# A 31-tap causal convolution on VectorE: 27 of its shifts made 1024 tokens wide, and its work spread anew beside the projections

## The chip, the cores and the metric

The program runs on one core of one Trainium2 chip. The metric is the device time of one execution in microseconds (us); of several executions the median counts. Engines are named as the profile names them: PE (TensorE products), PEld (its weight loads), DVE (VectorE), ACT (ScalarE), POOL (GpSimd), SP (SyncE, which here issues loads).

## The reference

The program computes a first block (a mixer of convolution, pooling and attention, then a mixture of experts) and a second block of two layers, on 1024 tokens of width 1024. The change touches the start of the first block alone:

```python
h = rms_norm(x, attn_norm_g)
z = h @ w_in
a_val, a_gate, p_in, q, k, v = split(z)
# convolution branch, 256 channels
u = a_val * sigmoid(a_gate)
y = depthwise_conv(u, w_dw, width=31, causal) + b_dw
y = silu(layer_norm(y, ln_g, ln_b))
y_conv = y @ w_pw + b_pw
# pooling branch, 256 channels: window sums of 2, 4, 8, 16 tokens
y_pool = pool_mixer(p_in)
# attention branch: q and k are normalised per head, then differential attention over q, k, v
mix = concat([y_conv, y_pool, attention(q, k, v)])
x = x + mix @ w_out
```

All matrix products are made of three products of high and low parts (a weight is split into `wh`, rounded, and `wl`, the rest; an activation into `mh` and `ml`).

## The kernel before

**Convolution.** Channels lie on the 128 partitions, tokens along the row, so the 256 channels are two tiles (j = 0, 1) of 128 x 1024. `conv_taps` (L638 to L658) walks over two halves of 512 tokens. A half begins with one `tensor_scalar` per channel tile (L650, shift 0 and bias); then 30 shifts follow, each a `scalar_tensor_tensor` per channel tile (L656) that adds u, moved by the shift and scaled by the tap's weight, to y. That is 4 instructions of L650 and 120 of L656, all on DVE. A shift with both its instructions is one stage of the generator: 62 stages in all.

**What is woven into what.** The program is written as generators. `_weave(main, side, steps)` (L262) takes `steps` steps of the side work after each step of the main work. Three parts of `build` matter (L2196 to L2203):

- `conv_pool`, through `group` and `partT` (L469), makes the first products `psT`: six weight tiles (two for the values of the convolution, two for its gate, two for the pooling input) by token blocks of 256, 256 and 512. The gate's sigmoid (L564 to L568, ACT and DVE in turn) and its product with the values (L635) give `u`.
- 14 stages of the taps are woven into the last part of those products, 1.3 after each step.
- `qkv` then makes the values `psV` (8 tiles of 24 products, L500) and the queries and keys `psQ` (n = 0 to 3, each 8 groups of 24 products, normalised by L777, L507 and L780, transposed as `psQT` by L787 and written by L796 and L797). Beside it, 3.4 steps after each of its steps, run the other 48 tap stages, with `pool_out` mixed into them at 0.55 steps each, and after both `conv_norm`.

`pool_out` makes the window sums with copies and adds on POOL (L669, L670) and their scaling on DVE (L676 to L680). `conv_norm` does the layer norm and silu of y in two halves: products with ones (`psM` L710, `psS` L578), then ACT and DVE in turn. `conv_out` splits y into `csh` (ACT, L450) and `csl` (L446 through `low`, on DVE or POOL) and multiplies it (`psC`); it is woven into the start of the attention (`psD`, L880 on DVE, exponentials L885 on ACT, L890 on POOL, L891 on DVE, `psAT` L901).

**Weights.** SP loads a weight tile into one of four raw buffers, ACT rounds it (`wh`, L450), and `low` (L442) takes the rest on DVE, every third one on POOL (`wl`, L446). The first group of queries reads four weight tiles; the low part of the second, `wl`, is its 15th product.

**The order.** The order of instructions on each engine is set when the program is built, by a scheduler that takes the written order and the dependencies; each engine then works through its queue strictly in that order. What stands behind a waiting instruction waits too.

Of the kernel before, what the change touches and what calls it, by code (L numbers as in the profile page):

```python
# [14 lines left out]
OP = mybir.AluOpType  # L15
# [241 lines left out]
def _run(g):  # L257
    for _ in g:
        pass


def _weave(main, side, steps=1.0):  # L262

    due = 0.0
    for _ in main:
        yield
        due += steps
        while due >= 1.0:
            due -= 1.0
            if next(side, _END) is not _END:  # L270
                yield
    yield from side


def _some(gen, n):

    for _ in range(n):
        if next(gen, _END) is _END:
            return
        yield  # L280


def _chain(*gens):
    for g in gens:
        yield from g
# [31 lines left out]
class _Kernel:  # L317
# [321 lines left out]
        yield from self.group(lead, [  # L639
            lambda t0, n, j=j, use=use: self.partT(("c", j), self.hm, use, t0, n=n) for j, use in enumerate(uses)])  # L640

    def conv_taps(self):

        nc = self.nc
        us = self.us
        ys = self.ys = [self.d("cy") for _ in range(2)]
        for half in range(2):
            lo, hi = 512 * half, 512 * half + 512
            for j in range(2):
                nc.vector.tensor_scalar(ys[j][:, lo:hi], us[j][:, lo:hi], self.col(("cw", j), 30), self.col("cb", j),  # L650
                                        op0=OP.mult, op1=OP.add)
            yield
            for sh in range(1, 31):
                a = max(lo, sh)
                for j in range(2):
                    nc.vector.scalar_tensor_tensor(ys[j][:, a:hi], us[j][:, a - sh:hi - sh], self.col(("cw", j), 30 - sh),  # L656
                                                   ys[j][:, a:hi], op0=OP.mult, op1=OP.add)
                yield  # L658

    def pool_out(self):  # L660
# [1357 lines left out]
    def second_layer(self, i, lead):  # L2018
# [6 lines left out]
        values = self.gla_v(i)  # L2025
        yield from _some(values, 8)
        yield from _weave(_chain(
            values, self.gla_gate(i, 1), self.gla_qk(i, 2), self.gla_qk(i, 3),
            self.gla_gate(i, 2), self.gla_gate(i, 3), self.mla_gate(i, 0), self.mla_gate(i, 1), self.mla_c(i, "ckv"),
            _weave(self.mla_c(i, "cq"), self.mla_norm(i), 0.5), self.mla_gate(i, 2), self.mla_gate(i, 3)),  # L2030
            heads, 1.06)
        self.hm = None
        self.ahead = 1
        yield from self.mla_rope_in(i)
        yield from _weave(self.mla_nope(i), _chain(self.rope(i), self.mla_factor(i)), 1.2)
        self.ahead = 0
        attention = self.mla_attention(i)
# [131 lines left out]
    def build(self):  # L2169
        nc = self.nc  # L2170
        keys = [("c", j) for j in range(6)]
        keys += [("cp",)] + [("v1", 0, kq) for kq in range(4)] + [("n1", n, kh) for n in range(4) for kh in range(2)]
        keys += [("o1", n, kq) for n in range(2) for kq in range(4)]
        keys += [("pp", 0, nh) for nh in range(2)]
        keys += [("m", p, g) for p in PLACES for g in range(6)]
        keys += [("pp", 1, nh) for nh in range(2)]
        for i in range(LAYERS):
            keys += [("k0", i), ("qk", i, 0), ("gg", i, 0), ("qk", i, 1)]
            keys += [("gv", i, 0, kq) for kq in range(4)]
            keys += [("gg", i, 1), ("qk", i, 2), ("qk", i, 3), ("gg", i, 2), ("gg", i, 3)]  # L2180
            keys += [("ga", i, 0), ("ga", i, 1)]
            keys += [("ckv", i, j) for j in range(2)] + [("cq", i, j) for j in range(3)]
            keys += [("ga", i, 2), ("ga", i, 3)]
            keys += [("uq", i, j) for j in (2, 0, 1)] + [("uk", i), ("uv", i)]
            keys += [(n, i, c, kq) for n in ("o2", "pg") for c in range(2) for kq in range(4)]
        self.order(keys)


        lead = self.first_in()
        lead.step()  # L2190
        lead.step()
        lead.step()
        self.pre(1)
        lead.step()
        self.pre(2)
        self.ahead = 2  # L2196
        first = self.conv_pool(lead)
        _run(_some(first, 6))
        self.lambdas()
        _run(_some(first, 7))  # L2200
        taps = self.conv_taps()
        _run(_weave(first, _some(taps, 14), 1.3))
        self.ahead = 1  # L2203
        _run(_weave(self.qkv(), _chain(_weave(taps, self.pool_out(), 0.55), self.conv_norm()), 3.4))
        if self.stop == "qkv":
            return
        self.ahead = 0
        self.spare_rows()
        attention = _weave(self.diff_attention(), self.conv_out(), 1.0)
        _run(_some(attention, 39))  # L2210
        self.router_setup()
        order = OUT_ORDER
        self.fill_ycp(order[0] // 2)

        def fill(t):
            n = order.index(t)
            if n % 2 == 0 and n < 6:
                self.fill_ycp(order[n + 2] // 2)
        self.pp = self.tc.dram_tile([LAYERS, S, D], F32, name="pp")
        self.later = []  # L2220
        side = self.ple_proj(0, 4)

        def products():
            self.pre(8)
            for half, t in self.out_proj(("o1",), self.io["x"], self.after_first, order, fill, True):
                if (half, t) == (1, order[5]):
                    self.rope_tables()
                    self.make_masks()
                if (half, t) == (0, order[6]):
                    self.choose_most()  # L2230
                if (half, t) == (1, order[-1]):
                    self.ple_load(0)
                    self.pre(1)
                if (half, t) == (0, order[-1]):
                    _run(_some(side, 1))
                yield
        _run(_weave(attention, products(), 1.0))
        self.route(lambda n: _run(_some(side, n)))
        experts = self.experts()
        next(experts)  # L2240
        _run(side)
        if self.stop == "route":
            return
        self.ahead = 0
        for u, n in experts:
            if u == 8:
                self.overflow_rows()
            if u == n - 4:
                self.ple_load(1)
            if u == n - 2:  # L2250
                self.ahead = 1
            if u == n - 1:
                outs = [self.d("ppo") for _ in range(NT)]
                for o in outs:
                    nc.gpsimd.memset(o[:, 0:1], 0.0)
                side = self.ple_proj(1, outs=outs)
                _run(_some(side, 2))
                self.pool_every = 3
        self.overflow()
        lead = self.second_in()  # L2260
        lead.step()
        _run(_some(side, 6))
        lead.step()
        lead.step()
        _run(_some(side, 3))
        lead.step()
        _run(_some(side, 3))
        lead.step()
        _run(_some(side, 2))
        if self.stop == "moe":  # L2270
            lead.need(NT)
            return

        self.x_in = self.x2
        for i in range(LAYERS):
            self.ahead = 2
            _run(self.layer_in(i, lead))
            _run(self.second_layer(i, lead))
            lead = self.lead
            if self.stop == f"l{i}":  # L2280
                return
# [28 lines left out]
```

## Time and profile before

| | us |
|---|---|
| median of 3 runs | 2265.68 (2257.85 to 2266.74) |
| the profiled execution, its own time | 2266.57 |
| its span in the profile | 2264.8 |
| PE busy | 2130.3 (94%) |
| DVE busy | 1488.8 (66%) |
| ACT busy | 1154.4 (51%) |
| POOL busy | 495.9 (22%) |

The span runs from the first to the last instruction that the profile shows; 1.8 us of the execution's time lie around it. The busy shares are averages over the whole program; the part that the change touches is the stretch from about 65 to 300 us of the span, some 10% of it.

### The profile page before, as it was taken

How to read it: one execution, taken by the hardware profiler on the slowest of the kernel's cores; microseconds unless marked ns; L12 is line 12 of the kernel's file. 1: busy time of each engine (PE TensorE's matmuls, PEld its weight loads, DVE VectorE, ACT ScalarE, POOL GpSimd, SP SyncE). 2: the span in 40 equal slices, each digit the busy share in tenths (PEclk: the TensorE clock that was granted, in tenths of full speed). 3: DMA queues.
4: the chain of work that ended last, by engine and by line, in shares of the span. 5: the costliest groups of instructions: out<-in, count | busy, mean ns of one | idle time of the engine just before them, and what ended most of it. 6: DMA issues, size and time to landing. Idle time of an engine off the chain costs nothing.

```text
span 2264.8 us, 31148 instructions
## 1 busy us (share of the span) xinstructions
PE 2130.3 (94%) x11660; PEld 1805.5 (80%) x11660; DVE 1488.8 (66%) x2534; ACT 1154.4 (51%) x2184; POOL 495.9 (22%) x431
## 2 busy tenths in 40 slices
PE   7989888998999989999899999999999989999998
PEld 7878777786887768887688988888877877898886
DVE  5995788577788733576756674566267665675455
ACT  5314778435677655354444553356354444554344
POOL 1320143202232211112322341101021232332100
PEclk9999999999999999999999999999999999999999
DMA  5101231638999971011022024444001113013343
GB/s 199 47 19 57 75 84 33 215 118 284 283 326 325 269 232 63 19 47 66 29 75 56 10 75 159 165 153 143 10 29 56 47 66 84 10 43 135 121 150 130
DMA packets 78446, 255.09 MB, mean 113 GB/s; under 512 B 9680, under 2 KB 16976, under 8 KB 78288
## 3 DMA queue, kind: packets, MB, share of 16 engines
q1 hardware_dynamic: 65024, 205.84, 26.2%
q0 software_dynamic: 10672, 38.00, 7.2%
q10 hardware_dynamic: 2592, 9.18, 1.1%
q8 instruction: 94, 1.54, 0.3%
q14 instruction: 64, 0.52, 0.1%
HBM read 183.51 MB, written 58.98 MB: 107 GB/s over the span
## 4 chain that ended last, share of the span: by engine, by line
PE 65%; DVE 18%; DMA 6%; ACT 5%; issue 4%; POOL 1%; POOLq 0%; DVEq 0%; SPq 0%; ACTq 0%
PE psR L500 19%; PE psT L469 14%; PE psS L459 6%; PE psO L459 5%; DVE cy L656 4%; PE psV L500 4%; DMA raw<-in_wm_dram 3%; PE psG L1292 3%; PE psQ L500 3%; PE psPT L1968 2%; DVE wl L446 2%; PE psY L459 2%; PE psX L549 1%; ACT wh L450 1%; PE psMV L459 1%
## 5 line engine op out<-in xcount | busy, mean ns | idle before, releaser
L469 PE MATMUL psT<-mh,wh 128*128 128x512 f32 (+1 forms) x784 | 292.4, 373 | 9.5 <-ACT k L1568 4.1
L469 PE MATMUL psT<-ml,wh 128*128 128x512 f32 (+1 forms) x784 | 288.7, 368 | 2.1 <-DVE ml L558 2.1
L469 PE MATMUL psT<-mh,wl 128*128 128x512 f32 (+1 forms) x784 | 287.7, 367 | 0.0
L446 DVE TENSOR_TENSOR wl<-raw,wh 128x1024 fp32r<-128x1024 f32 x171 | 222.6, 1308 | 54.1 <-ACT wh L450 52.1
L450 ACT ACTIVATE wh<-raw 128x1024 fp32r<-128x1024 f32 x205 | 214.8, 1055 | 67.0 <-DMA raw<-in_wm_dram 29.3
L469 PEld LDWEIGHTS psT<-mh,wh 128*128 128x128 f32 x784 | 153.1, 195 | 35.4 <-ACT k L1568 4.8
L446 POOL TENSOR_TENSOR wl<-raw,wh 128x1024 fp32r<-128x1024 f32 x34 | 87.7, 2581 | 415.4 <-ACT wh L450 370.7
L469 PEld LDWEIGHTS psT<-ml,wh 128*128 128x128 f32 x784 | 152.8, 195 | 24.8 <-DVE ml L558 3.1
L469 PEld LDWEIGHTS psT<-mh,wl 128*128 128x128 f32 x784 | 152.8, 195 | 23.1
L500 PE MATMUL psR<-wh,mixh 128*128 128x512 f32 x384 | 152.3, 397 | 2.6 <-DVE mpT L1973 1.7
L500 PE MATMUL psR<-wh,mixl 128*128 128x512 f32 x384 | 149.9, 390 | 0.9 <-POOL mixl L446 0.9
L500 PE MATMUL psR<-wl,mixh 128*128 128x512 f32 x384 | 149.9, 390 | 0.0
L1956 POOL TENSOR_SCALAR mp<-mp,mrr 128x512 f32<-128x512 f32 x128 | 92.6, 736 | 213.1 <-DVE mrr L1954 191.7
L1952 ACT ACTIVATE mp<-psS,mnm,rq 128x1024 f32<-128x1024 f32 x64 | 77.4, 1209 | 83.3 <-DVE mnm L1949 83.2
L500 PE MATMUL psR<-wl,mh 128*128 128x512 f32 (+1 forms) x264 | 101.3, 384 | 1.2 <-DVE wl L446 1.2
L500 PE MATMUL psR<-wh,mh 128*128 128x512 f32 (+1 forms) x264 | 102.0, 386 | 0.0
L500 PE MATMUL psR<-wh,ml 128*128 128x512 f32 (+1 forms) x264 | 101.0, 383 | 0.0
L557 ACT ACTIVATE mh<-psX 128x256 fp32r<-128x256 f32 (+1 forms) x144 | 60.9, 453 | 77.3 <-PE psX L549 72.3
L459 PEld LDWEIGHTS psO<-mpT,mv 128*128 128x128 f32 x768 | 96.4, 191 | 2.6
L1947 DVE TENSOR_REDUCE mmx<-psS 128x1 f32<-128x1024 f32 x64 | 78.1, 1220 | 29.1 <-PE psS L459 29.0
L459 PE MATMUL psO<-mpT,mv 128*128 128x256 f32 x768 | 97.1, 283 | 0.0
L987 DVE TENSOR_TENSOR xr<-psR,xr 128x512 f32<-128x512 f32 x48 | 33.0, 690 | 94.2 <-PE psR L500 78.6
(498 smaller groups left out, 5665.3 us busy)
## 6 DMA issues: line engine op xcount, KB each, us to landing
raw<-in_wg_dram SPq DMA_DIRECT2D x109, 512.0 KB, 3.5
raw<-in_wm_dram SPq DMA_DIRECT2D x96, 512.0 KB, 6.2
pp<-ppo ACTq DMA_DIRECT2D x16, 512.0 KB, 7.5
h<-xr SPq DMA_DIRECT2D x16, 512.0 KB, 2.8
xr<-h SPq DMA_DIRECT2D x16, 512.0 KB, 4.8
ppr<-pp SPq DMA_DIRECT2D x16, 512.0 KB, 5.8
xt<-in_x_dram SPq DMA_DIRECT2D x8, 512.0 KB, 11.2
xr<-in_x_dram SPq DMA_DIRECT2D x8, 512.0 KB
```

Source lines behind the costliest of these rows:

```text
L446: e.tensor_tensor(out, full, high.bitcast(F32), op=OP.subtract)
L450: self.nc.scalar.activation(h, src, AF.Copy)
L459: self.nc.tensor.matmul(out, a, b, start=j == 0, stop=j == n - 1)
L469: self.nc.tensor.matmul(ps, p[:, a], q, start=k == 0 and j == 0, stop=k == nk - 1 and j == 2)
L500: self.nc.tensor.matmul(out, p, q[:, b], start=k == 0 and j == 0, stop=k == 7 and j == 2)
L557: nc.scalar.activation(h, v, AF.Copy)
L656: nc.vector.scalar_tensor_tensor(ys[j][:, a:hi], us[j][:, a - sh:hi - sh], self.col(("cw", j), 30 - sh), ys[j][:, a:hi], op0=OP.mult, op1= ...
L1292: self.nc.tensor.matmul(pg, m[x][:, k], w[:, b], start=k == 0 and n == 0, stop=k == 7 and n == 2)
L1947: nc.vector.tensor_reduce(mx, ps, axis=AX.X, op=OP.max)
L1952: nc.scalar.activation(p, ps, AF.Exp, bias=nm, scale=self.rq[0][:, t:t + 1], accum_out=sm)
L1956: nc.gpsimd.tensor_scalar(p[:, b], p[:, b], rr, 1.0, op0=OP.mult, op1=OP.mult)
L1968: nc.tensor.transpose(pt[:, a, 128 * n:128 * n + 128], p[:, 256 * c + 128 * a:256 * c + 128 * a + 128], self.ident)
```

## The change

The taps of a half keep their 512 tokens only for shift 0 and the shifts 1 to 3. The 27 shifts 4 to 30 become one instruction each per channel tile, 1020 to 994 tokens wide, and each of these 54 instructions is a stage of its own. Only 4 stages (shift 0 to 3 of the first half) are woven into the first products, 0.4 after each step, instead of 14. All others lie beside `qkv`: 2.6 steps after each of its first 8 steps (the values) and 3.5 after each later one, with `pool_out` at 0.5.

```diff
 def _weave(main, side, steps=1.0):
 
     due = 0.0
-    for _ in main:
+    for n, _ in enumerate(main):
         yield
-        due += steps
+        due += steps(n) if callable(steps) else steps
...
-    def conv_taps(self):
+    def conv_taps(self, early):
...
-        for half in range(2):
-            lo, hi = 512 * half, 512 * half + 512
+
+        def tap(j, sh, lo, hi):
+            a = max(lo, sh)
+            nc.vector.scalar_tensor_tensor(ys[j][:, a:hi], us[j][:, a - sh:hi - sh], self.col(("cw", j), 30 - sh),
+                                           ys[j][:, a:hi], op0=OP.mult, op1=OP.add)
+        for lo, hi in ((0, 512), (512, 1024)):
...
-            for sh in range(1, 31):
-                a = max(lo, sh)
+            for sh in range(1, early):
                 for j in range(2):
...
+                    tap(j, sh, lo, hi)
+                yield
+        for sh in range(early, 31):
+            for j in range(2):
+                tap(j, sh, 0, 1024)
                 yield
...
-        taps = self.conv_taps()
-        _run(_weave(first, _some(taps, 14), 1.3))
+        taps = self.conv_taps(4)
+        _run(_weave(first, _some(taps, 4), 0.4))
         self.ahead = 1
-        _run(_weave(self.qkv(), _chain(_weave(taps, self.pool_out(), 0.55), self.conv_norm()), 3.4))
+        _run(_weave(self.qkv(), _chain(_weave(taps, self.pool_out(), 0.5), self.conv_norm()),
+                    lambda n: 2.6 if n < 8 else 3.5))
```

Lines of the changed kernel behind L640 stand six further on; its taps are L650 and its shift 0 is L654. Three places show what moves in the built order. In the names, `cy` is y, `wl` a weight's low part, `pd` and `ps` belong to the pooling, the number tells one buffer from another.

First, DVE beside the first products, around the gate's sigmoid (L565, L567, L635) of the last 512 tokens. Before:

```order
L656 SCALAR_TENSOR_TENSOR cy_738<-u_158,cols_85,cy_738 128x500
L565 TENSOR_SCALAR u_157<-u_157 128x512
L656 SCALAR_TENSOR_TENSOR cy_737<-u_157,cols_85,cy_737 128x499
L656 SCALAR_TENSOR_TENSOR cy_738<-u_158,cols_85,cy_738 128x499
L567 SCALAR_TENSOR_TENSOR u_157<-u_157,psT_771 128x512
L446 TENSOR_TENSOR wl_921<-raw_917,wh_919 128x1024
L446 TENSOR_TENSOR wl_927<-raw_923,wh_925 128x1024
```

With the change:

```order
L650 SCALAR_TENSOR_TENSOR cy_764<-u_158,cols_85,cy_764 128x509
L446 TENSOR_TENSOR wl_901<-raw_897,wh_899 128x1024
L446 TENSOR_TENSOR wl_907<-raw_903,wh_905 128x1024
L565 TENSOR_SCALAR u_157<-u_157 128x512
L567 SCALAR_TENSOR_TENSOR u_157<-u_157,psT_767 128x512
L635 TENSOR_TENSOR u_157<-aval_155,u_157 128x512
L654 TENSOR_SCALAR cy_763<-u_157,cols_85 128x512
```

Ahead of the gate stand 6 taps instead of 24, the two weight splits come before the gate, and nothing stands between the gate's steps.

Second, DVE around the two weight splits that the first queries need. Before:

```order
L656 SCALAR_TENSOR_TENSOR cy_737<-u_157,cols_85,cy_737 128x512
L676 SCALAR_TENSOR_TENSOR pd_969<-ps_1142,pin_160 64x1008
L680 TENSOR_TENSOR pd_969<-pf_1176,pin_160 64x16
L446 TENSOR_TENSOR wl_1218<-raw_1214,wh_1216 128x1024
L446 TENSOR_TENSOR wl_1224<-raw_1220,wh_1222 128x1024
L676 SCALAR_TENSOR_TENSOR pd_969<-ps_1209,pin_160 64x1008
L656 SCALAR_TENSOR_TENSOR cy_738<-u_158,cols_85,cy_738 128x512
```

With the change:

```order
L650 SCALAR_TENSOR_TENSOR cy_763<-u_157,cols_85,cy_763 128x1000
L446 TENSOR_TENSOR wl_1170<-raw_1166,wh_1168 128x1024
L446 TENSOR_TENSOR wl_1176<-raw_1172,wh_1174 128x1024
L682 SCALAR_TENSOR_TENSOR pd_975<-ps_1248,pin_160 64x1008
L650 SCALAR_TENSOR_TENSOR cy_764<-u_158,cols_85,cy_764 128x1005
L650 SCALAR_TENSOR_TENSOR cy_763<-u_157,cols_85,cy_763 128x999
L650 SCALAR_TENSOR_TENSOR cy_764<-u_158,cols_85,cy_764 128x1004
L783 TENSOR_REDUCE qss_1209<-qsq_1207 128x4
```

Between the gate's first L635 and these splits stand 2 of L654, 6 half-width and 36 wide taps (before, between the gate's L567 and the splits, 2 of L650 and 67 half-width taps), the last 17 of them without a break; behind the splits 18 wide taps are left (before 27 half-width ones), 13 of them ahead of the eighth query tile. One scaling of the pooling (L682, which reads a sum from POOL) moves from ahead of the splits to right behind them, and the two splits for n = 1 move to ahead of the eighth query tile.

Third, ACT at the end of `qkv`, where `conv_out` begins. Before, the second half of `conv_norm` has ended 27 rows earlier:

```order
L796 ACTIVATE ql_2325<-psQT_2667,cols_85 64x256
L796 ACTIVATE ql_2327<-psQT_2654,cols_85 64x256
L796 ACTIVATE qh_2326<-psQT_2667,cols_85 64x256
L796 ACTIVATE ql_2327<-psQT_2667,cols_85 64x256
L450 ACTIVATE csh_2707<-cy_737 128x1024
L450 ACTIVATE csh_2711<-cy_738 128x1024
L885 ACTIVATE at_2695,few_2689<-at_2695,few_2689 128x1024
```

With the change:

```order
L802 ACTIVATE ql_2240<-psQT_2585,cols_85 64x256
L566 ACTIVATE sg_2610<-sg_2610,sm_83 128x512
L566 ACTIVATE sg_2619<-sg_2619,sm_83 128x512
L568 ACTIVATE sg_2610<-sg_2610 128x512
L568 ACTIVATE sg_2619<-sg_2619 128x512
L891 ACTIVATE at_2641,few_2635<-at_2641,few_2635 128x1024
L891 ACTIVATE at_2648,few_2635<-at_2648,few_2635 128x1024
L450 ACTIVATE csh_2653<-cy_763 128x1024
L450 ACTIVATE csh_2657<-cy_764 128x1024
```

The silu of the second half (from L579 on) now stands among and behind the last key tiles, and the rounding of y, for which `psC` waits, stands behind it and behind the first attention unit's exponentials. On PE, `psC` stands behind the score products of two units, and ahead of the other units' scores and of all `psAT`; before, the first `psAT` stood behind the scores of four units and half those of two more. One of the two `csl` is on POOL before and after.

## Rows read from the trace of the kernel before

**Rows 1.** The page: span, and the chain that ended last, share by engine.

```profile
span 2264.8 us, 31148 instructions
PE 65%; DVE 18%; DMA 6%; ACT 5%; issue 4%; POOL 1%; POOLq 0%; DVEq 0%; SPq 0%; ACTq 0%
```

**Rows 2.** The same chain in order of time (start, length, what), from 66 to 184 us.

```profile
66.60 16.88 DVE cy L656 x23
...
183.88 7.24 PE psQ L500 x48
```

**Rows 3.** Stretches: sum, PE, PEld, DVE, ACT, POOL busy (instructions), PE clock granted, DMA.

```profile
140.00:160.00 20.00, 11.20 (x71) 10.65 (x70) 19.95 (x31) 1.60 (x5) 0.00 (x0) 0.74 0.15 53
160.00:184.00 24.00, 19.20 (x156) 18.31 (x155) 23.15 (x43) 9.22 (x30) 2.73 (x1) 1.00 0.00 1
184.00:240.00 56.00, 55.40 (x428) 53.17 (x427) 27.86 (x56) 31.18 (x76) 3.98 (x2) 0.97 0.16 57
240.00:256.00 16.00, 12.74 (x75) 9.34 (x74) 13.68 (x24) 13.74 (x30) 0.79 (x1) 1.00 0.22 67
276.00:300.00 24.00, 18.38 (x79) 13.58 (x78) 20.08 (x42) 15.13 (x28) 8.55 (x10) 0.93 0.42 110
```

**Rows 4.** Timeline of PE: start, length, instruction, idle before it and what ended it.

```profile
143.52 0.28 PE L500 MATMUL psQ<-wh,ml 128*128 128x256 f32 x1
152.60 0.58 PE L500 MATMUL psQ<-wl,mh 128*128 128x256 f32 x1 [8.80 <-DVE wl L446]
```

**Rows 5.** Timeline of DVE (touching rows of one line are merged), 60 to 184 us.

```profile
60.95 1.28 DVE L523 SCALAR_TENSOR_TENSOR junk<-xt,ss,grow 128x1024 f32<-128x1024 f32 x1 [1.88 <-ACT ss L507]
62.15 0.75 DVE L558 TENSOR_TENSOR ml<-psX,mh 128x256 fp32r<-128x256 f32 x2
...
85.04 0.67 DVE L567 SCALAR_TENSOR_TENSOR u<-u,psT 128x512 f32<-128x512 f32 x1
...
130.82 11.35 DVE L656 SCALAR_TENSOR_TENSOR cy<-u,cols,cy 128x512 f32<-128x512 f32 x17
142.09 0.16 DVE L679 TENSOR_TENSOR pf<-ps,sm 64x16 f32<-64x16 f32 x1
...
151.34 2.34 DVE L446 TENSOR_TENSOR wl<-raw,wh 128x1024 fp32r<-128x1024 f32 x2
...
182.97 0.42 DVE L780 TENSOR_TENSOR qn<-psQ,qss 128x256 f32<-128x256 f32 x1 [0.21 <-ACT qss L507]
```

**Rows 6.** Timeline of ACT at the gate of the last 512 tokens.

```profile
82.33 0.60 ACT L564 ACTIVATE u<-psT 128x512 f32<-128x512 f32 x1 [4.84 <-PE psT L469]
```

**Rows 7.** Timeline of POOL, 87 to 172 us, and of DVE at the last of these.

```profile
103.16 0.51 POOL L669 COPY ps<-ps 128x2 f32<-128x2 f32 x1
103.63 2.39 POOL L670 TENSOR_TENSOR ps<-ps 128x1022 f32<-128x1022 f32 x1
115.55 6.34 POOL L669 COPY ps<-ps 128x4 f32<-128x4 f32 x1 [9.53 <-DVE pf L679]
170.60 2.73 POOL L446 TENSOR_TENSOR pdl<-pd,pdh 128x1024 fp32r<-128x1024 f32 x1 [40.84 <-ACT pdh L450]
...
170.34 3.55 DVE L656 SCALAR_TENSOR_TENSOR cy<-u,cols,cy 128x512 f32<-128x512 f32 x2
```

**Rows 8.** Waits from 240 to 256 us: who waited for whom, total, times, longest.

```profile
PE psS L578 <- ACT sqs L577: 1.8, 1, 1.8
```

**Rows 9.** Timeline of ACT: the second half of the silu, then the end of `qkv`.

```profile
254.83 0.69 ACT L579 ACTIVATE cr<-psS,sm 128x512 f32<-128x512 f32 x1 [0.53 <-PE psS L578]
...
263.63 0.63 ACT L568 ACTIVATE sg<-sg 128x512 f32<-128x512 f32 x1 [0.17 <-DVE sg L567]
...
278.92 2.00 ACT L450 ACTIVATE csh<-cy 128x1024 fp32r<-128x1024 f32 x2
```

**Rows 10.** Timeline of PE from the last transposed keys to the first `psAT`.

```profile
274.89 0.44 PE L787 MATMUL psQT<-sq,qn 128*128 128x128 f32 x2 [1.31 <-DVE qn L780]
284.52 0.50 PE L459 MATMUL psC<-csl,wh 128*128 128x512 f32 x1 [0.76 <-DVE csl L446]
295.49 0.74 PE L901 MATMUL psAT<-sq,at 128*128 128x128 f32 x5 [0.67 <-ACT at L885]
```

More of the change, by code (lines that the diff above doesn't have):

```diff
@@ L652, in conv_taps @@
             yield
-            for sh in range(1, 31):
-                a = max(lo, sh)
+            for sh in range(1, early):
                 for j in range(2):
-                    nc.vector.scalar_tensor_tensor(ys[j][:, a:hi], us[j][:, a - sh:hi - sh], self.col(("cw", j), 30 - sh),
-                                                   ys[j][:, a:hi], op0=OP.mult, op1=OP.add)
+                    tap(j, sh, lo, hi)
[3 more added lines that the diff above has]
+                tap(j, sh, 0, 1024)
                 yield
```

## The prediction

> **What bounds the kernel now.** I read the page's shares first [rows 1]: the chain that ended last is 65% PE and 18% DVE, so a saving counts only where PE waits for it. The chain in order of time tells where that is [rows 2]: from 66.60 us it runs on DVE, through the taps, and from 183.88 us on PE, through the queries. The stretches show the same from the side of the engines [rows 3]. [...] From 184 us PE is full (55.40 of 56) and DVE half empty. The reason for the hole stands in PE's timeline [rows 4]: after 143.52 us the next product waits until 152.60 us, 8.80 us of it for `wl`, a weight split of 1.2 us that stands in DVE's queue behind the taps. So the question is when DVE reaches that split (151.34 us [rows 5]) and the eighth query tile (182.97 us [rows 5]).
>
> **What a tap costs.** Seventeen 512-column taps start from 130.82 us, and the next instruction starts at 142.09 us [rows 5]: 0.663 us each. For 1024 columns the trace has no tap, but the same instruction in the norm, which starts at 60.95 us with the next at 62.15 us [rows 5]: 1.20 us. A wide tap of 1020 to 994 columns is then 1.18 us on the mean (17 columns fewer, at (1.20 - 0.663) / 512 = 1 ns each), where its two halves took 0.663 + 0.64. That saves 0.13 us in 54 places, 6.8 us of DVE time. The unknown is bounded by nothing saved and by twice this. [...] The rows decide, and the sum goes by them.
>
> **Term 1, the way to the split.** Before, DVE ends the gate's L567 and works from 85.04 us to 151.34 us [rows 5]: 66.3 us. In this lie 67 half taps and 2 of L650, about 67 x 0.65 + 0.9 = 44.5 us. With the change there stand 36 wide taps, 6 half ones and 2 of shift 0: 42.5 + 4.0 + 0.9 = 47.4 us. That is more, because only 6 taps instead of 26 have been done before the gate ends: DVE will idle beside the first products, from about 72 us to 83 us, but for two weight splits. From the 66.3 us also go: these two splits (2.3), one pooling scaling (1.2), two gate steps that now lie before the start (1.2), and one wait for POOL (2.2) that falls into DVE's idle time. So 66.3 + 2.9 - 6.9 = 62.3 us. The start: the gate's first ACT step begins at 82.33 us [rows 6]; six steps of 0.33 to 0.72 us with hand-offs end at 86.3 us, and 1.0 us later if a weight's rounding, now ahead of it on ACT, is late. From 86.8 us the split is reached at 149.1 us: **-2.2 us** (bounds -6 and +1).
>
> **Term 2, to the eighth query.** Before: 182.97 - 151.34 = 31.6 us with 27 half taps (17.9 us). Now 13 wide taps (15.3 us), but two splits for n = 1 (2.3 us) and a second pooling scaling (1.2 us): 32.5 us, **+0.9 us**. In return n = 1 can start while PE waits for that tile: 14 products of 0.12 us stand there, against a pooling product of 0.69 us: **-1.0 us**. The stretch from 184 us has a mean clock of 0.97 [rows 3], 56 x 0.03 = 1.7 us; a shorter wait may save it, I take half: **-0.9 us** (0 to -1.7). The 5 wide taps that remain (5.9 us) lie beside n = 1, where DVE has 28 us free [rows 3]: nothing; without that cover they would cost 1.5 us.
>
> **Term 3, conv_norm inside qkv.** In 240 to 256 us PE loses 3.3 us [rows 3], 1.8 us of it because the product with ones stands right behind the squares on ACT [rows 8]. In the new order two to four groups of products lie between. **-2.0 us** (0 to -3.3).
>
> **Term 4, the end of qkv.** Before, the last transposes start at 274.89 us, the rounding of y at 278.92 us, the last waiting part of `psC` at 284.52 us, and the first `psAT` at 295.49 us [rows 9, 10]. Now the second half of the silu stands there on ACT. In its old place it took from 254.83 to 264.26 us [rows 9], 9.4 us, among query work that fills some 2.5 us; so the rounding comes about 7 us later relative to the last transposes, up to 9.4 us. PE waits for it in `psC`, with the scores of the later units and all `psAT` queued behind; DVE cannot work on those scores either. What covers: the first attention unit's own chain on ACT, DVE and POOL needs some 20 us before its `psAT`, in the old order as in the new, and PE is idle 5.6 us of 276 to 300 us anyway [rows 3]. Lower bound nothing, upper bound 9.4 us; the nearest row to the true state is PE's existing idle time, so I take what is left of 9.4 us after it: **+4 us**.
>
> Sum: -2.2 + 0.9 - 1.0 - 0.9 - 2.0 + 4.0 = -1.2 us against the profiled execution's own 2266.57 us, that is 2265.4 us. That execution lies 0.9 us above the median of the runs, so the forecast for the median is **2264.5 us**. About 0.5% (11.3 us) is what a measurement of this kernel can tell from no change; this is far inside it. Behind the attention's first units the order of work is as before, so I carry the shift unchanged to the end.
>
> **The rivals.**
>
> *The hole closes (faster).* The 62.3 us of term 1 still hold some 10.7 us in which DVE waits for POOL: with a POOL add of 2.4 us a tap pair takes 3.55 us instead of 1.33 [rows 7]. If POOL's adds fall where DVE waits anyway, DVE is at the split at 138.4 us, before PE asks at 143.5 us. Then the whole hole goes (-9.1 us), and the products behind it, which ran 4 us at the lower clock, give 2 us back. With the other terms, -11.1 - 1.0 - 2.0 + 4.0 = -10.1 us: 2255.6 us. For it: DVE idles early, with POOL free. Against it: the pooling input is not there before about 94 us, after which the queue is full of taps. A part of it (POOL's adds take half as many taps with them) would give -5 us.
>
> *The end of qkv costs all (slower).* Place: ACT between the last key tile and `psC`. Price: the whole 9.4 us of term 4, and the attention's units 3 to 6 come that much later because the attention keeps DVE and ACT near their limit, so PE's idle time absorbs nothing. It decides as soon as the exposed part is over 5.2 us, which is what terms 1 to 3 gain. If these fail too (the splits reached no earlier, 0 us, because DVE's idle time beside the first products eats the saving), the time is 2265.7 + 9.4 = 2275 us.
>
> *POOL is starved.* A copy of 2 columns on POOL took 0.51 us, but one of 4 columns 6.34 us [rows 7], while DVE ran ten taps without a break. In the new order 17 wide taps, 20 us, stand without a break ahead of the splits, and right behind these DVE's L682 waits for a POOL sum. If POOL gets no turn before, L682 waits for a copy and an add, 0.51 + 2.39 us [rows 7], with three taps and the first query's statistics behind it: +2.9 us, 2267.4 us. [...]
>
> *The change does not do what it says.* The wide tap could cost as much as its halves (a shifted destination of odd start). Then term 1 and 2 lose 49 x 0.13 = 6.4 us: 2270.9 us.
>
> **How the numbers follow.** Forecast 0.48 (2258 to 2271 us), the hole closes 0.26 (2251 to 2260 us), starvation 0.12, the end of qkv 0.09, no saving 0.05. Starvation and no saving stay inside 0.5% of before (2254.4 to 2277.0 us). A little under half of the first rival's cases (0.12) and a tail of the forecast (0.06) pass 2254.4 us: faster 0.18. Of the slow rival's, half pass 2277.0 us, with 0.02 from the forecast's tail: slower 0.07. Same 0.75. The range takes in most of the first rival's span at its lower end and the no-saving case, with the start of the slow one, at its upper: 2252 to 2273 us; the rest is tails.
>
> **What would show it.** Right: wide taps of about 1.28 us in the records, 1.18 us apart; DVE idle between about 72 and 83 us; the wait of `psQ` for `wl` still there, at 4 to 8 us; the chain leaving DVE for PE near 181 us; the last transposes 5 to 6 us earlier than 274.89 us; PE waiting in front of `psC`. Wrong: no wait for `wl` at all (the hole closes), L682 waiting for POOL over 2 us (starvation), the first `psAT` later than 295.49 us by several us (the slow rival), wide taps over 1.3 us apart (no saving), or a difference that arises behind 400 us, where I expect none.

## The result: 0.5% slower, and the profile after

| | before | with the change |
|---|---|---|
| median | 2261.56 us (8 runs, 2257.85 to 2266.74) | 2274.27 us (8 runs, 2268.94 to 2280.39) |
| ratio, with its 95% interval | | 1.0052 (1.0039 to 1.0065), +11.8 us |
| the profiled execution, its own time | 2266.57 us | 2277.64 us |

The forecast was 2264.5 us, with 2252 to 2273 us as its range; the change came out slower and above the range. One of the eleven executions of the best version below was slow (3006.91 us at a granted clock of 0.653); it is left out of its ratio.

The chain that ended last, on the page of the changed kernel (span 2275.9 us):

```profile
PE 50%; DVE 8%; issue 3%; ACT 2%; DMA 1%; POOL 1%; ACTq 0%; SPq 0%; DVEq 0%; POOLq 0%
```

This line can't be set against [rows 1]: its shares add up to 65%, because the chain of this trace can be followed back only to 814.9 us. It says nothing of the stretch that the change touches, and the sign "the chain leaving DVE for PE near 181 us" can't be read. The stretches of [rows 3], with the changed kernel (sum, PE, PEld, DVE, ACT, POOL busy, PE clock granted, DMA):

```profile
140.00:160.00 20.00, 14.51 (x101) 13.75 (x100) 18.08 (x16) 1.76 (x5) 15.26 (x4) 0.83 0.16 53
160.00:184.00 24.00, 18.48 (x125) 18.27 (x126) 23.51 (x36) 10.05 (x28) 3.25 (x1) 0.82 0.13 44
184.00:240.00 56.00, 50.88 (x384) 49.37 (x383) 27.04 (x54) 24.18 (x66) 2.41 (x1) 0.93 0.09 30
240.00:256.00 16.00, 14.69 (x113) 13.39 (x112) 9.69 (x19) 11.25 (x27) 2.36 (x1) 0.99 0.27 99
276.00:300.00 24.00, 13.97 (x39) 8.80 (x38) 18.80 (x31) 15.57 (x27) 6.24 (x6) 0.68 0.14 29
```

In 140 to 160 us PE gained 3.3 us and its clock went from 0.74 to 0.83. Then it lost: 160 to 184 us now runs at 0.82 instead of 1.00, 184 to 240 us has 4.5 us less PE busy time in it, and 276 to 300 us 4.4 us less at 0.68 instead of 0.93.

Where the time went is seen best if one product is followed through two traces. The table gives the start of the same PE instruction in a trace less its start in the trace of before; the shift that the 97th value product already has, ahead of the split, is taken off (-1.5 us with the change, -3.1 to +0.4 us in the other runs). The columns are named by the time before: the second group of queries (155), n = 1 (184), the keys (212, 233, 244, 261, 270), scores (315), transposes (336) and the output's products (495).

```
at (us before)   155    184    212    233    244    261    270    315    336    495
the change      -3.5   -1.0   -1.3   +3.2   +3.9   +1.0   +3.0  +13.8  +12.4  +13.4
```

So 3.5 us are won at the split, 2.5 of them are lost again in n = 0, 4.5 us are lost between 212 and 233 us, 2.9 won at the first half of the norm (244 to 261), 2.0 lost between 261 and 270, where four `psM` products of the norm's second half now stand, and **10.8 us are lost between the last keys and the scores** (270 to 315). From 495 us to the end the difference stays between 10 and 13.4 us.

How far the table carries: two later runs whose order is that of the change up to 233 us (`conv_out` later, half the norm left out) give the same shifts there within 0.3 us. But the traced executions lie off the medians of their runs, that of before 5.0 us above, that of the change 3.4 us above. So the table tells the place of a loss, and the medians tell whether the total moved.

PE's waits behind these steps:

```profile
147.64 0.58 PE L500 MATMUL psQ<-wl,mh 128*128 128x256 f32 x1 [5.32 <-DVE wl L446]
162.53 0.69 PE L793 MATMUL psQT<-sq,qn 128*128 128x128 f32 x2 [2.65 <-DVE qn L786]
180.95 0.41 PE L793 MATMUL psQT<-sq,qn 128*128 128x128 f32 x2 [3.00 <-DVE qn L786]
231.58 0.50 PE L459 MATMUL psP<-pdh,wh 128*128 128x512 f32 x1 [1.53 <-DVE qn L786]
234.55 0.58 PE L500 MATMUL psQ<-wh,mh 128*128 128x256 f32 x1 [2.00 <-DVE ql L803]
...
283.60 0.50 PE L870 MATMUL psD<-qh 128*128 128x512 f32 x1 [3.61 <-DVE few L886]
286.69 1.86 PE L870 MATMUL psD<-ql,qh 128*128 128x512 f32 x4 [2.00 <-DVE few L886]
291.76 1.22 PE L459 MATMUL psC<-csh,wh 128*128 128x512 f32 x2 [3.22 <-ACT csh L450]
```

The first line answers to the wait of 8.80 us in [rows 4]. The pair at 231 to 235 us has no counterpart before: three more products `psP` of the pooling now stand there among the keys. The last three, 8.8 us, stand where before has the 0.76 us of [rows 10] for `csl` and this wait:

```profile
279.71 0.79 PE L864 MATMUL psD<-qh 128*128 128x512 f32 x1 [2.53 <-DVE few L880]
```

ACT's timeline over the same place answers to [rows 9]:

```profile
277.96 0.69 ACT L579 ACTIVATE cr<-psS,sm 128x512 f32<-128x512 f32 x1 [0.86 <-PE psS L578]
...
287.27 1.23 ACT L568 ACTIVATE sg<-sg 128x512 f32<-128x512 f32 x2 [1.30 <-DVE sg L567]
288.41 1.13 ACT L891 ACTIVATE at<-at,few 128x1024 f32<-128x1024 f32 x1
...
290.67 1.99 ACT L450 ACTIVATE csh<-cy 128x1024 fp32r<-128x1024 f32 x2
```

The second half of the silu runs from 277.96 to 288.50 us, two exponentials follow, and the rounding of y starts at 290.67 instead of 278.92 us. Seen from the last transposes (275.76 us, 274.89 before) it has moved from 4.0 to 14.9 us behind them. PE waits, and its granted clock is 0.50 until the products `psC` are nearly done:

```profile
284.50:301.50 17.00, 10.58 (x24) 7.01 (x23) 12.11 (x18) 8.22 (x13) 6.75 (x7) 0.50 0.29 58
```

The 10.8 us can be split: the first `psC` starts 8.9 us later than the shift at 270 us; its 24 products then take 11.0 us from first to last start instead of 7.8, 3.1 us more, mostly at the clock of 0.50 (0.43 us apart from 296.42 to 301.12 us; 0.23 us apart at 1.00 before, from 286.24 to 289.19 us); 1.2 us come back up to 315 us. The first `psAT` starts at 302.97 instead of 295.49 us, the prediction's sign for its slow rival.

### The profile page after: what moved, and what is told of

It reads as the page before. It is cut to its first block, busy times and chain, and to the rows that moved or that the text cites. A ratio compares the mean times of both kernels' runs of the same rounds, so it can differ in the third digit from the quotient of the medians.

```text
span 2275.9 us, 31090 instructions
## 1 busy us (share of the span) xinstructions
PE 2141.1 (94%) x11660; PEld 1810.9 (80%) x11660; DVE 1478.5 (65%) x2480; ACT 1153.4 (51%) x2184; POOL 500.1 (22%) x431
## 4 chain that ended last, share of the span: by engine, by line
PE 50%; DVE 8%; issue 3%; ACT 2%; DMA 1%; POOL 1%; ACTq 0%; SPq 0%; DVEq 0%; POOLq 0%
PE psR L500 15%; PE psT L469 13%; PE psS L459 6%; PE psO L459 4%; PE psV L500 4%; PE psPT L1974 2%; PE psMV L459 1%; PE psX L549 1%; DVE B L1652 1%; DVE wl L446 1%; PE psA L1701 1%; DVE B L1653 1%; PE psDS L1726 1%; PE psA L1707 1%; DVE qd L1677 0%
```

## The experiments

Theory A: what costs is the second half of `conv_norm` at the end of `qkv`. Theory B: PE's queue makes the cost, as `psC` waits for y ahead of most scores. Theory C: the wide taps and their new spread cost, wherever the norm stands. Each run is set against runs of the kernel before on the same chip; a ratio of 1.0005 is 1.1 us.

**Parts of the change undone, one at a time.** First the norm where it was:

```diff
-                    lambda n: 2.6 if n < 8 else 3.5))
+                    lambda n: 2.6 if n < 8 else 3.5 if n < 18 else 7.0 if n < 22 else 3.4))
```

> The change, but the last taps and conv_norm are woven in faster from step 18 of qkv on, so that both halves of the norm stand among the key products as before the change. Theory A (the second half of the norm and silu at the end of qkv is what costs): 10 to 12 us less than the change, 2262 to 2265 us; the first psAT comes 12 us earlier than with the change. Theory C (the wide taps and their new spread cost, wherever the norm stands): no less than 2271 us. Theory D (half at the end of qkv, half among the queries): about 2268 us.

Measured: 2263.43 us, ratio 0.9995 (0.9978 to 1.0013), in theory A's range; the first `psAT` came 8.6 us earlier (294.41 us), not 12. In the table:

```
at (us before)   155    184    212    233    244    261    270    315    336    495
norm early      -3.5   -1.1   +0.5   +0.5   +0.5   +0.3   +0.3   +0.3   +0.5   +1.0
```

PE's order behind the first queries is now nearly that of before; three products of the pooling still stand later. The rounding of y starts at 277.83 us, and the stretch of 276 to 300 us is back at [rows 3]:

```profile
276.00:300.00 24.00, 18.29 (x82) 13.72 (x81) 20.21 (x45) 15.11 (x28) 8.51 (x10) 0.93 0.42 110
```

The whole loss goes with the place of the norm (and of the pooling's later products, which this edit moves too); theory C falls.

The old spread, with 17 shifts wide:

```diff
-        taps = self.conv_taps(4)
-        _run(_weave(first, _some(taps, 4), 0.4))
+        taps = self.conv_taps(14)
+        _run(_weave(first, _some(taps, 14), 1.3))
...
-        _run(_weave(self.qkv(), _chain(_weave(taps, self.pool_out(), 0.5), self.conv_norm()),
-                    lambda n: 2.6 if n < 8 else 3.5))
+        _run(_weave(self.qkv(), _chain(_weave(taps, self.pool_out(), 0.55), self.conv_norm()), 3.4))
```

> The old spread (14 stages beside the first products, 3.4 and 0.55), with only the shifts 14 to 30 made 1024 wide: the norm and the PE order stay where they were. Theory A: a gain of 34 x 0.13 = 4.4 us of DVE time, of which 2 to 4 us show: 2257 to 2260 us against 2261.6 before. Theory C: 2264 us or more, because a wide tap keeps a query's short steps waiting twice as long.

Measured: 2258.48 us, ratio 0.9979 (0.9962 to 0.9996). Widening by itself gains some 4.7 us (1 to 9 by the interval), which agrees with the saving per tap, 4.4 us; in the trace it shows from n = 1 on (-2.8 us at 184, -4.1 us at 212).

The new spread, with every tap 512 wide (`conv_taps(31)` in place of `conv_taps(4)`):

> The new spread with every tap 512 wide. Theory A: the late norm costs its 10 to 11 us, and DVE loses the saving of 54 x 0.13 = 6.8 us as well: 2277 to 2281 us. If the wide taps and not the spread are the cost (theory C): 2262 to 2266 us.

Measured: 2273.68 us, ratio 1.0040 (1.0020 to 1.0060), 3 us under the range of theory A and far above that of C. The loss at the end is there (+0.4 us at 270, +10.9 us at 315). But the wide taps saved nothing against the narrow ones. DVE's timeline of this run shows why; the lines are from the first products, then the taps ahead of the split:

```profile
74.34 4.01 DVE L650 SCALAR_TENSOR_TENSOR cy<-u,cols,cy 128x507 f32<-128x507 f32 x6
...
79.42 4.64 DVE L650 SCALAR_TENSOR_TENSOR cy<-u,cols,cy 128x504 f32<-128x504 f32 x7
...
127.99 19.97 DVE L650 SCALAR_TENSOR_TENSOR cy<-u,cols,cy 128x512 f32<-128x512 f32 x30
147.88 2.35 DVE L446 TENSOR_TENSOR wl<-raw,wh 128x1024 fp32r<-128x1024 f32 x2
```

And the changed kernel:

```profile
76.28 1.23 DVE L446 TENSOR_TENSOR wl<-raw,wh 128x1024 fp32r<-128x1024 f32 x1 [3.99 <-ACT wh L450]
82.25 2.23 DVE L565 TENSOR_SCALAR u<-u 128x512 f32<-128x512 f32 x1 [4.75 <-ACT u L564]
...
126.33 20.11 DVE L650 SCALAR_TENSOR_TENSOR cy<-u,cols,cy 128x1008 f32<-128x1008 f32 x17
146.36 2.36 DVE L446 TENSOR_TENSOR wl<-raw,wh 128x1024 fp32r<-128x1024 f32 x2
```

Half-wide taps of the first 512 tokens can run while the second half of `u` is not there, and the scheduler fetches them forward even where they are written behind the first products. A wide tap needs both halves. So the wide taps leave DVE idle for 8.7 us at 72 to 82 us, which eats their saving: both kernels reach the split 3.5 to 3.7 us earlier than before, counted from the values.

`conv_out` two steps later in the attention:

```diff
-        attention = _weave(self.diff_attention(), self.conv_out(), 1.0)
+        attention = _weave(self.diff_attention(), _chain(range(2), self.conv_out()), 1.0)
```

> The change, with conv_out begun two steps later in the attention: psC then stands behind the scores of four units and the rounding of y behind four exponentials. Theory B (PE's queue: psC waits for y, with all other scores and psAT behind it): 6 to 9 us less than the change, 2265 to 2268 us. Theory A (the silu's own work on ACT and DVE and the lower clock, wherever psC stands): at most 3 us less, 2271 to 2275 us.

Measured: 2274.08 us, ratio 1.0045 (1.0030 to 1.0060). The total speaks for A. The trace speaks in part for B, with a caution: its execution took 2269.07 us, the fastest of the ten and 5.0 us below their median.

```
at (us before)   270    315    336    495
the change      +3.0  +13.8  +12.4  +13.4
out later       +1.9   +6.8   +5.2  +10.4
```

With `psC` behind the scores of four units the attention loses 3.3 us from 270 to 336 us instead of 9.4. Up to the output's products (336 to 495) 5.2 us are lost again; one wait there is new (PE 2.4 us for `mixl` on DVE), the rest I have not resolved. In this trace, then, PE's queue carries most of the loss inside the attention; by the median of the runs moving `psC` gains nothing. Why is not shown.

**The suspected cost taken away.** The second half of the norm left out:

```diff
-        for half in range(2):
+        for half in range(1):
             b = slice(512 * half, 512 * half + 512)
             ps = self.mm("psM")
```

> The change with the layer norm and silu of the second 512 tokens left out (y goes into conv_out as the taps leave it there). Theory A (this half at the end of qkv costs the whole loss): 2262 to 2265 us, the first psAT within 3 us of the kernel before. If the late first half and the late psP cost as well: 2267 to 2270 us.

Measured: 2260.34 us, ratio 0.9989 (0.9976 to 1.0002), 2 us below theory A's range; +1.0 us at 270, 0.0 at 315. All that is lost behind 270 us is this half of the norm, and so is most of the 2.0 us between 261 and 270. Against the kernel before, the first half and the late `psP` nearly cancel: +3.6 us at 244, +0.6 us at 261. That doesn't make the late `psP` free, as the next run shows.

**The pooling.** Three runs with the change's or another spread. First the pooling sooner (`pool_out` at 0.7 instead of 0.5):

> The change with pool_out at 0.7 instead of 0.5, so that psP stands in PE's queue among the queries and the first keys as before. If the stop of PE at 230 to 240 us (4 us idle and 5 us at the lower clock) is a cost of the late psP that lasts: 3 to 5 us less than the change, 2269 to 2271 us. If the old order only lost the same later, at conv_norm's first half: within 2 us of the change, 2272 to 2276 us.

Measured: 2269.11 us, ratio 1.0018 (1.0004 to 1.0032).

```
at (us before)   155    184    212    233    244    261    270    315    336    495
pool sooner     -0.4   -0.4   +1.8   -0.7   -1.2   -2.6   -0.6   +9.9   +8.5   +9.3
```

The stop at 231 to 235 us is gone (one of 2.64 us for `qn` comes at 240.01 us) and the gain lasts up to 270 us, but the second group of queries starts 3.1 us later than with the change, for the wait for `wl` is 8.3 us. The late `psP` and POOL's place ahead of the split are two ends of one rate.

Then 14 narrow early stages with the change's rates (the lines of `conv_taps` and `_some` as in the run with 17 wide shifts):

> The change's rates beside qkv (2.6, 3.5 and 0.5), but 14 half-wide stages beside the first products at 1.3 and only the shifts 14 to 30 wide. The norm then ends 2.7 steps of qkv earlier than with the change, among the keys. Theory A: the whole loss of the end of qkv goes; with DVE's idle time beside the first products filled again: 2256 to 2260 us. If the rates beside the values cost by themselves: 2263 us or more.

Measured: 2263.39 us, ratio 1.0007 (0.9996 to 1.0018). The end of `qkv` costs nothing any more (+2.1 us at 270, +1.1 at 315), as theory A wants, yet the run is 3 us over the range, in that of the second case (the rates beside the values cost by themselves). `psP` stops PE here too, now with `psM` behind it (-4.4 us at 212, +2.9 at 233, +4.4 at 244), and here 2.1 us of it are left at 270.

Last the pooling held back behind the split, in the changed kernel:

```diff
-        _run(_weave(self.qkv(), _chain(_weave(taps, self.pool_out(), 0.5), self.conv_norm()),
+        _run(_weave(self.qkv(), _chain(_weave(taps, self.pool_out(), lambda n: 0.1 if n < 28 else 1.3), self.conv_norm()),
```

> The change, with pool_out held back (0.1 step for each of the first 28 tap stages, then 1.3): no add of POOL and no scaling of the pooling stands ahead of the first queries' weight splits, but two wide taps more. If POOL's adds are what keeps DVE from the splits (about 1.7 us for each of three or four taps, and two scalings of 1.2 us): DVE is there 6 us earlier than with the change, the wait for wl of 5.3 us goes, and, as the end of qkv stays as it is, the time is 2268 to 2272 us. If the same delays return among the first queries, where DVE is full: 2273 to 2277 us in spite of the hole that is gone.

Measured: 2263.94 us, ratio 1.0006 (0.9996 to 1.0016): 10 us less than the change and 4 us below the first case's range, though the end of `qkv` still costs its 11 us (-8.2 us at 270, +2.9 at 315).

```
at (us before)   155    184    212    233    244    261    270    315    336    495
pool behind    -10.1   -7.7   -7.1   -5.6   -7.3  -10.2   -8.2   +2.9   +1.5   +2.3
```

DVE's timeline shows 38 taps, nearly all wide, without a break, where the change had 36 with two scalings and three more adds of POOL among them:

```profile
97.32 43.42 DVE L650 SCALAR_TENSOR_TENSOR cy<-u,cols,cy 128x1017 f32<-128x1017 f32 x38
140.66 2.35 DVE L446 TENSOR_TENSOR wl<-raw,wh 128x1024 fp32r<-128x1024 f32 x2
```

PE no longer waits for `wl`, so the hole is closed. Two scalings with their small steps are 2.9 us; two wide taps more are 2.4 us; so of the 5.7 us some 5.2 us are left, which I put down to taps beside POOL's adds. The traces show some 3.3 us of it in two places: 2.25 us for a shift 0 at 96.97 us, 0.54 with the adds held back, and 2.84 us for a tap at 123.27 us, alone 1.27. Expected was that these delays might come back among the first queries. None did: from 155 to 184 us 2.4 us are lost, as with the change (2.5), and the lead over the change stays at 6.7 us. The rest of the 10 us comes between 212 and 244 us, where the second stop of PE (2.00 us in the change) and the clock of 0.50 behind it (234 to 240 us) don't occur (the clock is 1.00 from 185 to 240 us here); six `psP` stand there in this run too, and why they don't stop PE is not shown.

**A better version.** 14 early stages, the taps beside the values and the first queries fewer, the rest faster, the pooling at 0.7:

```diff
-        _run(_weave(self.qkv(), _chain(_weave(taps, self.pool_out(), 0.5), self.conv_norm()),
-                    lambda n: 2.6 if n < 8 else 3.5))
+        _run(_weave(self.qkv(), _chain(_weave(taps, self.pool_out(), 0.7), self.conv_norm()),
+                    lambda n: 2.6 if n < 16 else 5.0 if n < 22 else 3.4))
```

> As the run with 14 early stages, but fewer taps beside the values and the first queries (2.6 for 16 steps), the rest beside n = 1 and the first keys (5.0), where DVE is half free, and pool_out at 0.7. If what is left of the loss is DVE's place at the first wl and in n = 0: 2251 to 2256 us. If the taps in n = 1 make PE wait for qn instead: 2258 to 2263 us.

Measured: 2256.49 us, ratio 0.9967 (0.9956 to 0.9979), 0.5 us above the better case; but the wait for `wl` is still 9.3 us, and what is won comes behind it (+0.5 us at 155, -4.3 us at 261). The same with the pooling held back (`lambda n: 0.1 if n < 24 else 1.3` for 0.7):

> The best version so far (14 early stages, 2.6 for 16 steps, then 5.0) with pool_out held back behind the first queries' splits (0.1 for 24 tap stages, then 1.3). If POOL's adds ahead of the splits are its remaining cost: the 9.3 us wait for wl falls to 2 to 4 us, and the time to 2249 to 2254 us. If they only move into the first queries: 2255 to 2259 us.

Measured: 2252.70 us, ratio 0.9963 (0.9950 to 0.9976): the best median, though by the ratios not told apart from the one before. Its wait for `wl`, and the stretches:

```profile
142.44 0.39 PE L500 MATMUL psQ<-wl,mh 128*128 128x256 f32 x1 [1.77 <-DVE wl L446]
```

```profile
140.00:160.00 20.00, 15.00 (x124) 14.57 (x123) 19.79 (x24) 3.69 (x14) 15.66 (x6) 1.00 0.16 54
160.00:184.00 24.00, 20.03 (x165) 19.41 (x164) 17.05 (x30) 10.03 (x30) 7.33 (x6) 1.00 0.14 45
```

The clock is 1.00 through both stretches (0.74 and 1.00 before, 0.83 and 0.82 with the change), with a wait of PE for `qn` of 3.23 us in the first (at 155.98 us). And with fewer steps beside the values (1.2 for 8, 3.0 up to 16, then 6.0; pooling at 0.7):

> The best version so far with fewer steps beside the values (1.2 instead of 2.6 for 8 steps, then 3.0, then 6.0); two scalings of the pooling instead of three stand ahead of the splits. If the number of steps beside the values sets the time of the splits: the wait for wl falls by 3 us or more and the time to 2250 to 2254 us. If the scheduler brings the taps forward in any case: within 2 us of 2256 us.

Measured: 2262.09 us, ratio 1.0001 (0.9990 to 1.0012): neither case. 100 half taps' worth stood ahead of the split as against 98, so the scheduler does bring the taps forward in any case; but the wait for `wl` fell only from 9.3 to 7.2 us, because a sum on POOL (1.89 us from 144.86 us) now fell right on the splits (two of them took 4.07 us from 144.89 us instead of 2.35), n = 0 and 1 lost what that gave, and the keys lost 3 us more (-0.5 us at 261, -4.3 in the run with 2.6).

## Why the prediction was wrong

The forecast was -1.2 us. At 495 us the trace of the change is 13.4 us behind, less the common shift of 1.5 us. By the prediction's terms: -1.0 us for terms 1 and 2 (forecast -3.2), +2.0 for term 3 (forecast -2.0), +12.8 for term 4 with the 2.0 us of its `psM` (forecast +4.0), and -0.4 behind it.

**The taps and the split (term 1): right.** Seventeen wide taps took (146.36 - 126.33) / 17 = 1.18 us each, as forecast. DVE idled beside the first products, and reached the split at 146.36 us, 3.5 us earlier once the common shift of 1.5 us is taken off; the forecast was 2.2 us. The parts were off in opposite directions: the taps behind the gate began at 87.39 us (forecast 86.8, without the shift), and from there DVE needed 59.0 us (forecast 62.3). Two rows were read a little off: at 85.04 us L567 starts and does not end, and the tap pair of 3.55 us stood beside a POOL instruction of 2.73 us, not an add of 2.4.

**To the eighth query (term 2): wrong sign.** The forecast was 32.5 us of DVE's time from the split to the eighth `qn`; it took 182.21 - 146.36 = 35.9 us. The 3.4 us more are POOL's. L682 waited 1.92 us for its sum, and three taps beside POOL's next add took 5.7 us (151.76 to 157.48) instead of 3 x 1.18:

```profile
151.76 5.79 DVE L650 SCALAR_TENSOR_TENSOR cy<-u,cols,cy 128x1005 f32<-128x1005 f32 x3
157.48 0.40 DVE L783 TENSOR_REDUCE qss<-qsq 128x4 f32<-128x256 f32 x1
...
182.21 0.42 DVE L786 TENSOR_TENSOR qn<-psQ,qss 128x256 f32<-128x256 f32 x1
```

```profile
151.92 3.40 POOL L676 TENSOR_TENSOR ps<-ps 128x1016 f32<-128x1016 f32 x1
```

Before, six adds of POOL stood ahead of the split; with the change four do, and term 2 had nothing for the other two. This is the place of the starvation rival (chance 0.12), at some 4 us on DVE instead of its 2.9. PE felt it in the middle, with waits for `qn` of 2.65 and 3.00 us. Of the 3.5 us won 1.0 was left at 184 us, and the -1.0 and -0.9 us of term 2 didn't come. The granted clock fell there, but that is not what cost: the same products, from the second group of queries to n = 1, in the change, with `conv_out` later and with half the norm left out:

```profile
149.91:181.09 31.18, 25.49 (x184) 24.84 (x182) 29.96 (x40) 10.71 (x30) 8.59 (x4) 0.87 0.09 27
148.41:179.45 31.04, 23.26 (x183) 21.97 (x182) 30.12 (x40) 10.58 (x30) 7.74 (x4) 0.99 0.09 28
148.50:179.53 31.03, 23.40 (x183) 22.11 (x182) 30.09 (x40) 10.59 (x30) 7.76 (x4) 0.98 0.08 28
```

The order is the same in all three; at 0.87, 0.99 and 0.98 of the clock they took the same time, with DVE full.

**conv_norm inside qkv (term 3): right in its own size, but a part was missing.** The first half of the norm gained 2.9 us (forecast 2.0). Overlooked: the lower rate of `pool_out` moves three of the twelve products `psP` from the queries to the keys. Between 212 and 233 us 4.5 us are lost, in waits of 1.21, 1.53 and 2.00 us; the wait of 1.53 us for `qn` is there with the pooling held back too, where a key product stands behind it and no `psP`, so not all of the loss is `psP`. I had costed the move of the pooling's scalings on DVE and not that of its products on PE.

**The end of qkv (term 4): the step that failed.** The mechanism was the forecast one and its place too, but not its size: +4 us forecast with 9.4 as upper bound, 10.8 us measured. The step was "what is left of 9.4 us after PE's existing idle time". That idle time covered nothing of the 8.9 us by which the first `psC` came later. It was itself a wait of the same chain, for `few` and `csl` from DVE (2.53 and 0.76 us before); with the change the chain begins later and the waits grow to 8.8 us. Two things stood outside the sum: the rounding of y came 10.9 us later (the bound of 9.4 left out the two exponentials between the silu and it, 288.41 to 290.67 us), and `psC` took 3.1 us longer, with a clock of 0.50 from 284.5 to 301.5 us (before 1.00 from 284.5 to 295.5 us), for which term 4 had nothing. So the slow rival (chance 0.09, 2275 us) describes the time and most of the way to it; its condition that the splits come no earlier did not hold, the gain of the splits was lost behind them instead. That its number fits so well is in part luck.

**The rivals on POOL.** "The hole closes" went by POOL's adds, and its size for the hole was about right: with the adds behind the split the wait of 5.32 us went, and the second group of queries came 10.1 us earlier than before (forecast 9.1 for the hole). Its total of -10.1 us is another sum, with the end of `qkv` at +4, and was not reached (+1.4 us by the ratio). But nothing in the change closed the hole; it took a run of its own. A wide tap that met an add of POOL (1.89 us from 123.16 us) took 2.84 us in its record (at 123.27 us), alone 1.27. Which of the two gets its turn first is taken up in the last section. The rival's 2 us for the clock are near what the trace of before shows: the products behind the hole started 0.21 us apart up to 156.39 us, at a granted clock of 0.50 (152 to 156 us), and 0.12 us apart from 156.87 us on, at 1.00 (157 to 160 us); over seventeen products that is some 1.6 us.

**The doubt about wide taps** was not borne out: they save 0.13 us each, with an odd start or an even one (1.24 us at 157.81 us from column 21 and at 159.31 us from column 22), and 0.2% where DVE has no new idle time (17 wide shifts in the old spread).

## What to carry to other kernels

When stages are moved along a queue, follow the last consumer of what now comes last: here half a norm, in steps of under a microsecond each, moved to where no products were left to cover it, cost 10.8 us where the moved taps had won 3.5. An idle stretch of the engine that waits was no cushion here for a step that feeds the same chain. And before an operation is made wider, look at when its inputs are there: the narrow form may be filling time that the wide one can't.

## What was not expected of the hardware

In the changed kernel a POOL instruction that came up amid a row of DVE's taps was not done before the row had ended: a copy of four columns, which elsewhere took 0.19 us (160.47 us in the best version), took 12.07 us, through eight taps and both weight splits, and ended when DVE waited for the sum behind it:

```profile
136.70 12.07 POOL L675 COPY ps<-ps 128x4 f32<-128x4 f32 x1 [11.66 <-issue]
148.72 1.88 POOL L676 TENSOR_TENSOR ps<-ps 128x1020 f32<-128x1020 f32 x1
```

```profile
150.64 1.20 DVE L682 SCALAR_TENSOR_TENSOR pd<-ps,pin 64x1008 f32<-64x1008 f32 x1 [1.92 <-POOL ps L676]
```

Copies of four or eight columns took 10.40, 11.85 and 12.54 us in three other runs (17 wide shifts in the old spread, every tap narrow, and the first better version). In [rows 7] one had taken 6.34 us, to 121.89 us, with DVE's taps running to 121.77 us; I had not read it as a wait that lasts to the end of a row.

It is no rule for every POOL instruction. Before the change, three copies and three adds of POOL got their turns between 97.31 and 106.02 us, each after about one tap (a copy of two columns 0.51 us, an add 2.39 us, [rows 7]; in the best version as little as 0.18 us at 157.30 us and 1.88 us at 148.13 us), in the midst of this row without a break:

```profile
95.42 18.81 DVE L656 SCALAR_TENSOR_TENSOR cy<-u,cols,cy 128x496 f32<-128x496 f32 x19
```

What decides who gets the next turn is not shown.
